# Weight sums spread over the products, a second out-projection in another product order, and mixing six steps behind its norm

## Chip, cores and metric

The kernel runs on one core of one Trainium2 chip. The metric is device time in microseconds (us); the time before is the median of three runs.

## What is computed

One decoder layer over 2048 tokens of width 1024, all in float32, and a final RMSNorm:

```python
h = rms_norm(x, norm_mix)
C, B, a, u, v, gA, gB = split(h @ w_in)                 # seven segments of 1024
y_a = B * causal_depthwise_conv(C * a, conv_w)
y_b = chunked_spatial_gating(gelu(u), gelu(v), ...)     # u * (tril(w_s) @ LN(v) + b) in chunks of 128
x = x + (sigmoid(gA) * y_a + sigmoid(gB) * y_b) @ w_out
h = rms_norm(x, norm_mlp)
x = x + square(relu(h @ w_ff1)) @ w_ff2
out = rms_norm(x, final_norm)
```

## The kernel before

**Tiling.** The tokens are two blocks of 1024. Every large product is done with one level of a Strassen-Winograd scheme: two by two quarters, seven products named 1 to 7 instead of eight. Each operand is split into a rounded part and a rest, and three matmuls of 128x128 against 512 columns stand for one exact product. A *step* is 12 such matmuls. For a product, sums of quarters of the weights (b11, b12, b21, b22) and of the activations are needed: those of the weights are made on VectorE (DVE) by `weight_sums` (L328), those of the activations by the jobs that write `h1d`, `md`, `h2d` and `hidd` to DRAM.

**Stages.** Per block: v projection (32 steps, `v_steps` L530), the other six segments (168 steps, `in_steps` L584). Then the out projection of block 0 and block 1 (28 steps each, `out_steps` L786), FF1 of both (112 each, `ff1_steps` L816) and FF2 of both (112 each, `ff2_steps` L850): 904 steps. `weave` (L997) interleaves the last four steps of a stage with the first four of the next. Here v.24 stands for step 24 of the v stage, out1 for the out projection of block 1, out0 for that of block 0.

**Order.** The order of TensorE (PE) and SyncE (SP, which issues the loads) is the program's; DVE, ScalarE (ACT) and GpSimd (POOL) are put in an order by the scheduler when the kernel is built, and then run their queues in that order. `drive` (L315) issues the loads of a step eight steps ahead and its preparation three steps ahead; jobs hung on a step by `at` (L974) come just before its matmuls. What stands in `with soon()` (L168) gets a priority 400 instructions earlier: weight sums, the splitting of weights into a unit (`wu`, four buffers) and the reading of PSUM banks. The splitting of activations (`hold<-rq`, `hold<-big`) has no such priority.

**Row products** (`row_steps` L684, used by out and FF2): nk steps per product (4 in out, 8 in each half of FF2), order `ROW_ORDER = "1265734"`. Products 1, 6, 7 and 4 add up in one set of four PSUM banks; product 2 has a set of its own; 5 and 3 share one in out0 and FF2 and have one each in out1 (`free`). After the last step of a product `read` (L739) adds the banks to rows of `x1`; a row that has all its sums is written to `x1d` by `finish`. PSUM has eight banks; the transposes and the mixing take from the same eight. The two weight quarters rows of a step are loaded with products 1 and 2, and product 6 makes all four weight sums.

**Jobs around it.** `ln_jobs` (L493) has `norm(i)`, the LayerNorm of 128 tokens of v and its split, and `mix(i, q)`, two groups of four matmuls (L461) on the result with reads by DVE (L521, L522); `at_mixes` (L989) hangs them on steps of v and of in. `h2_jobs(0)` (L1041, L1065) makes the normalised, transposed and summed input of block 0's FF1 during out1: `load(i)` of a row from `x1d`, `begin(i)` (square on ACT, power on POOL, scale on ACT), `turned(i)` (8 transposes on PE, L243, 8 evictions on ACT, L247), `sums(r)` (four sums on DVE into two tiles of the pool `extra`, which has two, and seven writes by POOL to `h2d`). FF1 of block 0 loads `h2d` from out1.20 on (L1057). Tiles of `hold` have fixed places named by letters; the rows `x1` of block 1 lie in places "5" (rows 0 to 3) and "3" (rows 4 to 7), and the first quarters of FF1 want all places "1" to "7" again (`quarters`, L280).

Of the kernel before, what the change touches and what calls it, by code (L numbers as in the profile page):

```python
# [38 lines left out]
def hybrid_block_kernel(  # L39
# [75 lines left out]
    def hf(dt=F32):  # L115
        return half.tile([P, HB], dt, tag="hf", name=nm("hf"))
# [21 lines left out]
    def sub(o, a, b):  # L138
        nc.vector.tensor_tensor(o, a, b, ALU.subtract)  # L139
# [11 lines left out]
    def split_new(src):  # L151
        u = wtile()
        split(u[:, 0, :], u[:, 1, :], src)
        return u
# [170 lines left out]
                f()  # L325
            st["run"]()

    def weight_sums(p, raw, st, after_2):  # L328

        b11, b12, b21, b22 = raw
        if p == "6":
            t = st["t"] = hf()
            sub(b11, b12, b11)
            sub(t, b22, b11)
            sub(b12, b22, b12)
            if after_2:
                sub(b21, b21, t)  # L340
        if p == "4" and not after_2:
            sub(st["t"], b21, st["t"])
        t = st.get("t")
        return {
            "1": b11, "6": t, "7": b12, "4": b21 if after_2 else t, "2": b21, "5": b11, "3": b22,
        }[p]

    def pair_steps(hq, cols, sink, done=None):

        raw, units, st = [], {}, {}

        def load():
            for n in range(2):
                for k in range(2):
                    t = rq()
                    src = cols[n][k * HB : (k + 1) * HB, :]  # L360
                    nc.sync.dma_start(
                        out=t.rearrange("p (k c) -> p k c", k=CH),
                        in_=src.rearrange("(k p) c -> p k c", p=P),
                    )
                    raw.append(t)

        def prep(p):
            b11, b21, b12, b22 = raw
            with soon():
                units[p] = split_new(weight_sums(p, (b11, b12, b21, b22), st, False))  # L370

        def run(p):
            first = p in "125"
            if first:
                st[GROUP[p]] = bank()
            ps = st[GROUP[p]]
            u, h = units.pop(p), hq[p]
            for k in range(CH):
                passes(
                    ps,  # L380
                    lambda a: u[:, a, k * P : (k + 1) * P],
                    lambda b: h[:, b, k, :],
                    first and k == 0,
                    k == CH - 1,
                    not first,
                )
            with soon():
                if p in "167":
                    st["s" + p] = hf()
                    copy(st["s" + p], ps)  # L390
                    return
                m, n = QUARTER[p]
                sink(m, n, ps, {"2": st["s1"], "3": st["s6"], "5": st["s7"], "4": None}[p])
            if p == ORDER[-1] and done is not None:
                done()

        return {
            p: step(load if p == "1" else nothing, lambda p=p: prep(p), lambda p=p: run(p))
            for p in ORDER
        }  # L400
# [281 lines left out]


    def row_steps(  # L684
        a_src, w, rows_of, nk, i0, x1, places, finish, free=False, late=False
    ):


# [3 lines left out]


        wrows, hid, banks, units, hraw = ({}, {}), {}, {}, {}, {}
        np_ = (nk + CH - 1) // CH

        def load(p, n):
            if p in "12":
                e = "12".index(p)
                if n % CH == 0:  # L700
                    wrows[e][n // CH] = held(places[e][n // CH], F32)
                r0 = rows_of(i0 + n)[e]
                nc.sync.dma_start(out=wrows[e][n // CH][:, n % CH, :], in_=w[r0 : r0 + P, :])
            t = rq()
            nc.sync.dma_start(out=t, in_=a_src[p][:, i0 + n, :])
            hraw[p, n] = t

        def prep(p, n):
            if n % CH == 0:
                hid[p, n // CH] = held(places[2]())  # L710
            h = hid[p, n // CH]
            split(h[:, 0, n % CH, :], h[:, 1, n % CH, :], hraw.pop((p, n)))
            w1 = wrows[0][n // CH][:, n % CH, :]
            raw = (w1[:, lo], w1[:, hi], None, None)
            if p != "1":
                w2 = wrows[1][n // CH][:, n % CH, :]
                raw = raw[:2] + (w2[:, lo], w2[:, hi])
            with soon():
                units[p, n] = split_new(weight_sums(p, raw, {}, True))

        def run(p, n):
            first = p in ("1253" if free else "125")
# [14 lines left out]
                )  # L737

            def read(r):  # L739
                for m, c in ROW_QUARTERS[p] if free or p != "5" else ((1, 1),):  # L740
                    t = x1[r + m * CH][:, c * HB : (c + 1) * HB]
                    with soon():
                        add(t, banks[p][r], t)
                    if p in "2734":
                        finish(r + m * CH, c)

            if late and p == "4" and n >= nk - CH:
# [15 lines left out]
                lambda p=p, n=n: prep(p, n),  # L763
                lambda p=p, n=n: run(p, n),
            )
            for p in ROW_ORDER
            for n in range(nk)
        ]

# [7 lines left out]
    def rotate(names):  # L777
        k = [0]

        def nxt():  # L780
            k[0] += 1
            return names[(k[0] - 1) % len(names)]

        return nxt

    def out_steps(blk, w_at, nxt, rows_at, free):  # L786
        x1, halves = [None] * (2 * CH), set()

        def finish(i, h):
# [11 lines left out]
            x1,  # L801
            (w_at[0], w_at[1], nxt),
            finish,
            free=free,
        )
        r0 = blk * BLK
# [167 lines left out]
    def at(steps, n, f):  # L974
        steps[n]["before"].append(f)
# [10 lines left out]
            if n % 2:  # L986
                at(steps, s + lag + 1, lambda r=n // 2: sums(r))

    def at_mixes(steps, n0, every, lag, jobs_of):  # L989
        for i in range(CH):  # L990
            at(steps, n0 + i * every, lambda i=i: jobs_of()[0](i))
            for q in range(2):
                at(steps, n0 + i * every + lag + q, lambda i=i, q=q: jobs_of()[1](i, q))

    phases = []

# [9 lines left out]
    for blk in blocks:  # L1006
# [16 lines left out]
        else:  # L1023
# [3 lines left out]
            for n, p in enumerate("675"):  # L1027
                bring(v[19 + 3 * n], *quarters(hq, h1d[blk], p))
            bring(inn[5], *quarters(hq, h1d[blk], "3"))
        at_mixes(v, 17, 3, 4, lambda blk=blk: late[blk, 0])  # L1030
        at_mixes(inn, 4, 2, 4, lambda blk=blk: late[blk, 1])
        if blk + 1 < NBLK:
            r0 = (blk + 1) * BLK
            jobs = quarter_jobs(
# [6 lines left out]
    def h2_jobs(blk):  # L1041
# [3 lines left out]

    nxt_g = rotate("673")
    outs = [
        out_steps(0, "16", rotate("7425"), (None, None), False),
        out_steps(1, "74", rotate("3162162"), ("5", "3"), True),
    ]  # L1050
    ff1s = [ff1_steps(blk, hqs[blk]) for blk in blocks]
    for blk in blocks:
# [10 lines left out]
                bring(s, load, prep)  # L1063

    load, begin, turned, sums = h2_jobs(0)  # L1065
    for n, s in enumerate((9, 9, 10, 11, 17, 17, 18, 19)):
        i = n // 2 + CH * (n % 2)
        at(outs[1], (2, 4, 4, 5, 8, 9, 10, 10)[n], lambda i=i: load(i))
        at(outs[1], (4, 6, 6, 7, 12, 12, 13, 13)[n], lambda i=i: begin(i))
        at(outs[1], s, lambda i=i: turned(i))  # L1070
        if n % 2:
            at(outs[1], s, lambda r=n // 2: sums(r))
    at_jobs(ff1s[0], 16, 10, 6, h2_jobs(1))
    at(outs[0], 8, no_more_z)
    for ph in outs + ff1s + [ff2_steps(blk, nxt_g) for blk in blocks]:
# [40 lines left out]
```

## Time and profile before

| | us |
|---|---|
| median of three runs | 2619.2 (2619.05 to 2620.46) |
| the profiled execution | 2617.14 |
| its span, first to last instruction | 2615.4 |
| PE busy | 2556.8 |
| DVE busy | 1853.1 |
| ACT busy | 1331.2 |
| POOL busy | 355.1 |
| granted TensorE clock, mean | 0.991 |

A busy time is the union of an engine's instructions; matmuls are pipelined and their ends are modelled. The granted clock is 1.00 at 2.4 GHz and 0.5 at 1.2 GHz, and a mean between them says how much of a stretch was at the lower one.

### The profile page before, as it was taken

How to read it: one execution, taken by the hardware profiler on the slowest of the kernel's cores; microseconds unless marked ns; L12 is line 12 of the kernel's file. 1: busy time of each engine (PE TensorE's matmuls, PEld its weight loads, DVE VectorE, ACT ScalarE, POOL GpSimd, SP SyncE). 2: the span in 40 equal slices, each digit the busy share in tenths (PEclk: the TensorE clock that was granted, in tenths of full speed). 3: DMA queues.
4: the chain of work that ended last, by engine and by line, in shares of the span. 5: the costliest groups of instructions: out<-in, count | busy, mean ns of one | idle time of the engine just before them, and what ended most of it. 6: DMA issues, size and time to landing. Idle time of an engine off the chain costs nothing.

```text
span 2615.4 us, 33276 instructions
## 1 busy us (share of the span) xinstructions
PE 2556.8 (98%) x11405; PEld 2112.7 (81%) x11405; DVE 1853.1 (71%) x3061; ACT 1331.2 (51%) x2377; POOL 355.1 (14%) x628
## 2 busy tenths in 40 slices
PE   9999999999999999999989999999999999999998
PEld 7778888888878888887768878888887888878887
DVE  6886776766887666777776666866668677685865
ACT  7444554445544344443666666755555444544444
POOL 1330111100330000000222223121121000000001
PEclk9999999999999999999999999999999999999999
DMA  6322344336332222354975555844449364563532
GB/s 218 93 76 86 122 133 136 121 111 223 113 93 85 69 89 69 101 184 141 370 256 195 190 185 197 274 150 158 145 149 338 129 209 122 204 242 118 183 127 77
DMA packets 291053, 410.65 MB, mean 157 GB/s; under 512 B 22804, under 2 KB 187716, under 8 KB 290884
## 3 DMA queue, kind: packets, MB, share of 16 engines
q1 hardware_dynamic: 247700, 276.90, 33.0%
q0 software_dynamic: 38576, 123.24, 13.1%
q10 hardware_dynamic: 4608, 8.39, 0.9%
q8 instruction: 89, 1.46, 0.2%
q14 instruction: 80, 0.66, 0.1%
HBM read 285.24 MB, written 123.21 MB: 156 GB/s over the span
## 4 chain that ended last, share of the span: by engine, by line
PE 32%; issue 9%; DMA 3%; DVE 3%; POOL 3%; ACT 1%; POOLq 0%; SPq 0%; ACTq 0%; DVEq 0%
PE ps L159 32%; POOL hidd L837 2%; DVE hold L139 1%; DMA rq<-in_w_ff_dram 1%; DMA rq<-hidd 1%; DVE wu L139 1%; DVE big L136 0%; DVE hf L139 0%; DMA h2d<-extra 0%; POOL h2d L260 0%; DMA hidd<-big 0%; DMA rq<-md 0%; PE ps L243 0%; DMA big<-h2d 0%; POOL st L873 0%
## 5 line engine op out<-in xcount | busy, mean ns | idle before, releaser
L159 PE MATMUL ps<-hold,wu 128*128 128x512 f32 x6720 | 1541.7, 390 | 11.7 <-ACT hf L145 8.9
L159 PEld LDWEIGHTS ps<-hold,wu 128*128 128x128 f32 x6720 | 1262.0, 188 | 277.1 <-ACT hf L145 11.5
L159 PE MATMUL ps<-wu,hold 128*128 128x512 f32 x4128 | 959.8, 393 | 18.8 <-DVE hold L139 12.4
L159 PEld LDWEIGHTS ps<-wu,hold 128*128 128x128 f32 x4128 | 779.6, 190 | 184.4 <-DVE hold L139 14.9
L139 DVE TENSOR_TENSOR wu<-rq,wu 128x512 fp32r<-128x512 f32 x464 | 319.9, 690 | 196.8 <-ACT wu L145 192.8
L145 ACT ACTIVATE wu<-rq 128x512 fp32r<-128x512 f32 x464 | 290.9, 627 | 308.3 <-PE ps L159 190.4
L145 ACT ACTIVATE wu<-hold 128x512 fp32r<-128x512 f32 x240 | 151.0, 631 | 280.3 <-PE ps L159 274.1
L145 ACT ACTIVATE hf<-ps 128x512 f32<-128x512 f32 x240 | 143.1, 596 | 262.5 <-PE ps L159 261.1
L139 DVE TENSOR_TENSOR wu<-hold,wu 128x512 fp32r<-128x512 f32 x240 | 165.4, 690 | 153.2 <-ACT wu L145 153.0
L139 DVE TENSOR_TENSOR wu<-hf,wu 128x512 fp32r<-128x512 f32 x200 | 137.8, 689 | 158.0 <-ACT wu L145 157.6
L145 ACT ACTIVATE wu<-hf 128x512 fp32r<-128x512 f32 x200 | 125.7, 629 | 174.1 <-PE ps L159 121.6
L139 DVE TENSOR_TENSOR hold<-rq,hold 128x512 fp32r<-128x512 f32 x280 | 181.2, 687 | 10.4 <-ACT hold L145 10.4
L837 POOL DMA_DIRECT2D hidd<-big x224 | 121.4, 542 | 459.5 <-ACT big L825 370.9
L145 ACT ACTIVATE hold<-rq 128x512 fp32r<-128x512 f32 x280 | 158.0, 619 | 48.7 <-DMA rq<-md 32.9
L136 DVE TENSOR_TENSOR big<-ps,hf 128x512 f32<-128x512 f32 x120 | 82.7, 689 | 60.1 <-PE ps L159 59.8
L139 DVE TENSOR_TENSOR rq<-rq,rq 128x512 f32<-128x512 f32 x160 | 110.2, 689 | 3.4 <-DMA rq<-in_w_ff_dram 0.3
L136 DVE TENSOR_TENSOR hf<-ps,hf 128x512 f32<-128x512 f32 x96 | 66.3, 690 | 62.1 <-PE ps L159 61.8
L873 POOL TENSOR_TENSOR st<-st,mhalf 128x1 f32<-128x1 f32 x16 | 14.5, 908 | 586.6 <-DVE st L872 586.6
L660 POOL DMA_DIRECT2D md<-big x56 | 30.5, 546 | 464.9 <-DVE big L136 454.1
L136 DVE TENSOR_TENSOR big<-ps,big 128x512 f32<-128x512 f32 (+1 forms) x148 | 90.5, 670 | 4.3 <-PE ps L159 2.9
L524 POOL DMA_DIRECT2D mixd<-hf x128 | 71.0, 555 | 115.5 <-DVE hf L522 63.8
L139 DVE TENSOR_TENSOR big<-big,big 128x512 f32<-128x512 f32 (+1 forms) x109 | 83.9, 771 | 1.9 <-ACT big L145 0.3
(108 smaller groups left out, 1585.0 us busy)
## 6 DMA issues: line engine op xcount, KB each, us to landing
rq<-in_w_in_dram SPq DMA_DIRECT2D x256, 256.0 KB, 2.9
hidd<-big POOLq DMA_DIRECT2D x224, 256.0 KB, 2.6
rq<-hidd SPq DMA_DIRECT2D x224, 256.0 KB, 3.9
rq<-in_w_ff_dram SPq DMA_DIRECT2D x128, 256.0 KB, 3.2
hold<-in_w_ff_dram SPq DMA_DIRECT2D x64, 512.0 KB, 6.6
big<-x1d SPq DMA_DIRECT2D x32, 512.0 KB, 7.3
md<-big POOLq DMA_DIRECT2D x56, 256.0 KB, 4.9
rq<-md SPq DMA_DIRECT2D x56, 256.0 KB, 8.5
```

The costliest lines, as they stand in the source:

```text
L136: nc.vector.tensor_tensor(o, a, b, ALU.add)
L139: nc.vector.tensor_tensor(o, a, b, ALU.subtract)
L145: nc.scalar.activation(o, a, AF.Copy)
L159: nc.tensor.matmul(ps, lhsT=stat_of(a), rhs=mov_of(b), start=first and n == 0, stop=last and n == 2, skip_group_check=goes_on,)
L524: nc.gpsimd.dma_start(out=mixd[blk][h + e][:, c0 : c0 + P], in_=o)
L660: nc.gpsimd.dma_start(out=md[blk][p][:, j, :], in_=src)
L837: nc.gpsimd.dma_start(out=hidd[blk][p][:, i, :], in_=src)
L873: nc.gpsimd.tensor_tensor(r, v, mhalf, ALU.pow)
```

## The change

Three things. `weight_sums` gets the order of the products and makes each sum at the product that first wants it: in ROW_ORDER b12-b11 moves from product 6 to 2, and b22-b12 from 6 to 7; in the order `ORDER = "1674253"` (the pairs of in and FF1, which had it before) b22-b12 moves from 6 to 7. out1 runs in ORDER instead of ROW_ORDER: its four products on one set of banks come first and one behind the other, the second weight row is loaded with product 6, and product 4 makes one sum more per step, since no tile is kept between products. Which product ends a quarter of the rows is worked out from the order. With it the jobs of `h2_jobs(0)` get other steps: rows are turned one per step, all sums are hung on out1.11 to 15 instead of 9 to 19. In v the norms go from steps 17, 20, 23, 26 to 16, 17, 18, 19, and the mixes from 21, 24, 27, 30 (and the next step of each) to 20, 22, 26, 28; in `in` the norms stay at 4, 6, 8, 10 and the mixes go from 8, 10, 12, 14 to 10, 12, 14, 16.

```diff
-    def weight_sums(p, raw, st, after_2):
+    def weight_sums(p, raw, st, order):
         b11, b12, b21, b22 = raw
-        if p == "6":
-            t = st["t"] = hf()
+        after_2 = order.index("2") < order.index("6")
+        if p == ("2" if after_2 else "6"):
             sub(b11, b12, b11)
-            sub(t, b22, b11)
+        if p == "6" or (p == "4" and "t" not in st and not after_2):
+            st["t"] = hf()
+            sub(st["t"], b22, b11)
+        if p == "6" and after_2:
+            sub(b21, b21, st["t"])
+        if p == "7":
             sub(b12, b22, b12)
-            if after_2:
-                sub(b21, b21, t)
...
     def row_steps(
-        a_src, w, rows_of, nk, i0, x1, places, finish, free=False, late=False
+        a_src, w, rows_of, nk, i0, x1, places, finish, order=ROW_ORDER, free=False, late=False
     ):
...
+        quarter_of = {p: q if free or p != "5" else ((1, 1),) for p, q in ROW_QUARTERS.items()}
+        adds = {
+            (m, c): [p for p in ORDER if (m, c) in quarter_of[p]]
+            for m in range(2)
+            for c in range(2)
+        }
         def load(p, n):
-            if p in "12":
-                e = "12".index(p)
+            if p in order[:2]:
+                e = order.index(p)
...
-                units[p, n] = split_new(weight_sums(p, raw, {}, True))
+                units[p, n] = split_new(weight_sums(p, raw, {}, order))
...
-                    if p in "2734":
+                    if all(p == q or order.index(q) < order.index(p) for q in adds[m, c]):
                         finish(r + m * CH, c)
...
-    def at_mixes(steps, n0, every, lag, jobs_of):
+    def at_mixes(steps, norms, mixes, jobs_of):
         for i in range(CH):
-            at(steps, n0 + i * every, lambda i=i: jobs_of()[0](i))
+            at(steps, norms[i], lambda i=i: jobs_of()[0](i))
             for q in range(2):
-                at(steps, n0 + i * every + lag + q, lambda i=i, q=q: jobs_of()[1](i, q))
+                at(steps, mixes[i] + q, lambda i=i, q=q: jobs_of()[1](i, q))
...
-        at_mixes(v, 17, 3, 4, lambda blk=blk: late[blk, 0])
-        at_mixes(inn, 4, 2, 4, lambda blk=blk: late[blk, 1])
+        at_mixes(v, (16, 17, 18, 19), (20, 22, 26, 28), lambda blk=blk: late[blk, 0])
+        at_mixes(inn, (4, 6, 8, 10), (10, 12, 14, 16), lambda blk=blk: late[blk, 1])
...
-        out_steps(0, "16", rotate("7425"), (None, None), False),
-        out_steps(1, "74", rotate("3162162"), ("5", "3"), True),
+        out_steps(0, "16", rotate("7425"), (None, None), ROW_ORDER, False),
+        out_steps(1, "74", rotate("3162162"), ("5", "3"), ORDER, True),
...
-    for n, s in enumerate((9, 9, 10, 11, 17, 17, 18, 19)):
-        i = n // 2 + CH * (n % 2)
-        at(outs[1], (2, 4, 4, 5, 8, 9, 10, 10)[n], lambda i=i: load(i))
-        at(outs[1], (4, 6, 6, 7, 12, 12, 13, 13)[n], lambda i=i: begin(i))
-        at(outs[1], s, lambda i=i: turned(i))
-        if n % 2:
-            at(outs[1], s, lambda r=n // 2: sums(r))
+    for i in range(2 * CH):
+        at(outs[1], (2, 2, 3, 3, 4, 5, 6, 7)[i], lambda i=i: load(i))
+        at(outs[1], (4, 4, 5, 5, 7, 8, 9, 10)[i], lambda i=i: begin(i))
+        at(outs[1], (6, 7, 8, 9, 11, 12, 13, 15)[i], lambda i=i: turned(i))
+        if i >= CH:
+            at(outs[1], (11, 12, 13, 15)[i - CH], lambda r=i - CH: sums(r))
```

## Rows read from the trace of the kernel before

**Rows 1.** The page, part 1: busy us (share of the span) and instructions of each engine.

```profile
PE 2556.8 (98%) x11405; PEld 2112.7 (81%) x11405; DVE 1853.1 (71%) x3061; ACT 1331.2 (51%) x2377; POOL 355.1 (14%) x628
```

**Rows 2.** Timeline of PE, undisturbed: start, us, instruction, count; FF2, then v of block 0.

```profile
2023.10 257.15 PE L159 MATMUL ps<-wu,hold 128*128 128x512 f32 x1133 [0.27 <-DVE hold L139]
...
82.80 1.11 PE L461 MATMUL ps<-big,big 128*128 128x256 f32 x8
83.75 2.91 PE L159 MATMUL ps<-wu,hold 128*128 128x512 f32 x12
```

**Rows 3.** Windows: stretch, length, busy us (instructions) by engine, clock, DMA share, GB/s.

```profile
93.00:107.00 14.00, 10.89 (x43) 8.91 (x42) 10.27 (x26) 6.44 (x15) 4.94 (x9) 0.76 0.32 94
171.00:191.00 20.00, 16.84 (x68) 13.71 (x69) 16.26 (x43) 6.67 (x10) 7.90 (x15) 0.83 0.19 59
745.00:762.00 17.00, 14.18 (x67) 11.57 (x68) 15.86 (x42) 6.32 (x10) 7.59 (x14) 1.00 0.21 67
1193.00:1206.00 13.00, 9.43 (x30) 7.23 (x29) 10.10 (x17) 2.52 (x4) 3.24 (x6) 0.74 0.77 240
1263.00:1270.00 7.00, 4.82 (x15) 3.81 (x15) 7.00 (x13) 3.86 (x7) 2.13 (x4) 0.76 1.03 401
1277.00:1296.00 19.00, 14.69 (x78) 11.60 (x77) 11.55 (x22) 17.84 (x46) 6.29 (x10) 1.00 1.03 402
1308.00:1333.00 25.00, 19.88 (x95) 15.87 (x93) 17.40 (x32) 21.81 (x53) 8.14 (x13) 0.93 0.50 160
1344.00:1380.00 36.00, 28.73 (x111) 22.56 (x110) 28.74 (x39) 18.19 (x26) 4.28 (x8) 0.91 0.99 351
2005.00:2027.00 22.00, 18.45 (x78) 13.96 (x77) 21.97 (x37) 8.36 (x15) 1.62 (x3) 1.00 0.90 330
2316.00:2332.00 16.00, 10.70 (x39) 8.34 (x38) 13.79 (x27) 6.74 (x14) 1.79 (x2) 0.79 0.66 218
```

**Rows 4.** Timeline of PE where it waited: in brackets us idle and what ended it.

```profile
98.52 2.93 PE L159 MATMUL ps<-wu,hold 128*128 128x512 f32 x6 [3.11 <-ACT big L569]
...
172.66 0.38 PE L461 MATMUL ps<-big,big 128*128 128x256 f32 x1 [1.73 <-ACT big L145]
174.17 1.86 PE L461 MATMUL ps<-big,big 128*128 128x256 f32 x7 [1.13 <-DVE big L139]
...
1265.29 15.46 PE L159 MATMUL ps<-wu,hold 128*128 128x512 f32 x60 [2.18 <-DVE big L136]
...
1370.03 10.32 PE L159 MATMUL ps<-hold,wu 128*128 128x512 f32 x37 [3.17 <-ACT hf L145]
...
2322.49 22.73 PE L159 MATMUL ps<-wu,hold 128*128 128x512 f32 x90 [5.30 <-DVE hold L139]
```

**Rows 5.** Timeline of DVE: reads of banks and a sum in out1, splits in FF2.

```profile
1264.46 2.48 DVE L136 TENSOR_TENSOR big<-ps,big 128x512 f32<-128x512 f32 x4
...
1341.21 0.69 DVE L139 TENSOR_TENSOR extra<-big,big 128x512 f32<-128x512 f32 x1 [3.28 <-DMA h2d<-extra]
...
2321.76 3.09 DVE L139 TENSOR_TENSOR hold<-rq,hold 128x512 fp32r<-128x512 f32 x5
```

**Rows 6.** Groups of DVE, 2294 to 2322 us: busy, mean ns, idle before them.

```profile
L139 DVE TENSOR_TENSOR hold<-hold,hold 128x512 f32<-128x512 f32 x6 | 4.1, 688 | 0.0
```

**Rows 7.** Groups of DVE, 1164 to 1198 us.

```profile
L139 DVE TENSOR_TENSOR hold<-hold,hold 128x512 f32<-128x512 f32 x2 | 1.4, 694 | 0.0
```

**Rows 8.** Timeline of ACT before the wait at 98.52.

```profile
96.84 1.06 ACT L145 ACTIVATE big<-big 128x1024 fp32r<-128x1024 f32 x1 [1.50 <-DVE big L504]
```

**Rows 9.** Waits of the SP queue, 1240 to 1380 us: total, times, longest.

```profile
SPq L288 <- DMA h2d<-big: 20.8, 2, 20.5
```

**Rows 10.** DMA issues: count, KB each, median us to landing.

```profile
x1d<-hold POOLq DMA_DIRECT2D x8, 512.0 KB, 8.5
```

**Rows 11.** The chain of waits, 1300 to 1375 us: start, us, what.

```profile
1333.72 7.47 DMA h2d<-extra
```

More of the change, by code (lines that the diff above doesn't have):

```diff
@@ L369, in prep @@
             with soon():
-                units[p] = split_new(weight_sums(p, (b11, b12, b21, b22), st, False))
+                units[p] = split_new(weight_sums(p, (b11, b12, b21, b22), st, ORDER))
         def run(p):
@@ L684, in row_steps @@
     def row_steps(
-        a_src, w, rows_of, nk, i0, x1, places, finish, free=False, late=False
+        a_src, w, rows_of, nk, i0, x1, places, finish, order=ROW_ORDER, free=False, late=False
     ):
         wrows, hid, banks, units, hraw = ({}, {}), {}, {}, {}, {}
-        np_ = (nk + CH - 1) // CH
+        quarter_of = {p: q if free or p != "5" else ((1, 1),) for p, q in ROW_QUARTERS.items()}
[4 more added lines that the diff above has]
+        }
         def load(p, n):
-            if p in "12":
-                e = "12".index(p)
+            if p in order[:2]:
+                e = order.index(p)
                 if n % CH == 0:
@@ L739, in read @@
             def read(r):
-                for m, c in ROW_QUARTERS[p] if free or p != "5" else ((1, 1),):
+                for m, c in quarter_of[p]:
                     t = x1[r + m * CH][:, c * HB : (c + 1) * HB]
@@ L765, in row_steps @@
             )
-            for p in ROW_ORDER
+            for p in order
             for n in range(nk)
@@ L784, in rotate, with out_steps @@
         return nxt
-    def out_steps(blk, w_at, nxt, rows_at, free):
+    def out_steps(blk, w_at, nxt, rows_at, order, free):
         x1, halves = [None] * (2 * CH), set()
@@ L803, in out_steps @@
             finish,
+            order=order,
             free=free,
```

## Prediction

> **What bounds the kernel now.** I read the page's part 1 first: PE is busy 98% of the span, DVE 71%, ACT 51% [rows 1]. So time can only come out of PE's gaps and out of the stretches in which its clock was lower. The undisturbed pace is in PE's timeline: 1133 matmuls in 257.15 us, 0.227 us each, so a step of 12 takes 2.72 us; one mix adds 0.95 us (82.80 to 83.75) [rows 2]. 904 steps at that pace are some 2460 us.
>
> Then I went through PE's waits and laid a window over each place at which a step took longer than that; apart from the first 55 us and from 2.9 us in FF1 of block 0, which the change doesn't touch, they all lie where the change works [rows 3, 4]. What a window lost is its length less its matmuls at 0.227 us, where it has nothing else: out0 13 - 30 x 0.227 = 6.2; start of out1's second product 7 - 15 x 0.227 = 3.6; out1 into FF1 36 - 111 x 0.227 = 10.8; FF2 of block 0 22 - 78 x 0.227 = 4.3; FF2 of block 1 16 - 39 x 0.227 = 7.1. In the last one idle is 5.3 us and the clock's share (1 - 0.79) x 16 = 3.4, so about 54% of the clock's share came on top of the idle time. With that for the mixed windows: v of block 0 3.1 + 0.54 x 3.4 = 4.9; mixing in block 0 3.2 + 1.8 = 5.0; in block 1 2.8; out1's first turns 4.3; its later turns 5.1 + 0.9 = 6.0. Together 55 us, which is all that this change could give.
>
> **FF2 sums (11.4 us).** In the window of block 1 PE waits 5.30 us for a split of activations on DVE [rows 4]. DVE has no idle time there; it makes weight sums of product 6, which have priority, while product 2 wants its activations, and the five splits come only at 2321.76 [rows 5]. The change adds and drops no sum in FF2. It puts one of four per step behind: 8 per half. Six of those lie in the 28 us before the splits [rows 6]; DVE starts one every 0.60 us (2.48 us for four, [rows 5]), so the splits come 3.6 us earlier, 4.8 if the two before count as well. A wait of 0.5 to 1.7 us is left of 5.3. I take no fall of the clock with it, since out1's first turns idle 4.3 us in 19 at a clock of 1.00 [rows 3]; 6.0 of 7.1 us return. The same 3.6 us cover the 3.55 us idle of block 0 (22 - 18.45): 4.0 of 4.3. **Gain 10**; bounds 0 (the scheduler makes the sums as early as before, since they keep their priority) and 11.4.
>
> **out0 (6.2 us).** It gets the same spreading, but with four steps per product everything lies within the 400 instructions of priority, and in the trace only two of the moved sums lie in the 34 us before its wait [rows 7]. Two times 0.60 us leave, if at all. **Gain 1**; bounds -2 (the sums fall into the crunch) and 6.2.
>
> **Mixing in `in` (7.8 us).** Mix 3 waits for the split of its norm, first on ACT, then on DVE: 1.73 + 1.13 us [rows 4]. The norms stay; mix 3 goes two steps later, which is 2 x (2.72 + 0.95) less the two mixes that no longer lie before it, 2 x 0.95: 5.4 us later, and DVE has two mixes fewer to read before that norm. 2.9 us were missing. What is late next: the reads of the last mixes now meet the convolution on DVE, which is busy 16.3 of 20 and 15.9 of 17 us there [rows 3]. **Gain 6.5**; bounds 2 and 7.8.
>
> **Mixing in v (4.9 us).** At v.24 PE waits 3.11 us for evictions on ACT (L569) [rows 4]; ACT's queue had the split of norm 2 before them, itself waiting for DVE [rows 8]. With norm 2 at step 18 that obstacle is gone. But four mixes and all four norms now come before step 24 instead of three mixes and three norms, and DVE is nearly full there (10.3 of 14 us with the wait in it, [rows 3]); the eight tiles that four norms want at once also don't fit beside the rest of the pool of 12, so norm 2 waits for mix 0 anyway. **Gain 1** for both blocks; bounds -7 (both blocks wait at step 24 for reads on DVE) and 4.9.
>
> **out1 (24.7 us).** Its parts:
> - *Second product.* Before, product 2 waited for four banks of out0, 2.18 us until a read by DVE [rows 4]. Now product 6 goes on in the banks of product 1, so it wants the four reads behind those: 2.39 us later [rows 5], less the two sums that leave (1.2). Costs 1.5 more; bounds -4 and +3.6.
> - *Two more hand-overs* (6 to 7, 7 to 4) on the same banks, which there were not before. PE comes back to the first bank 2.0 us (9 matmuls) after finishing it, 2.9 with a turn between, and an add takes 0.6: free if DVE's queue is short, else up to 3.6 each as above. I take 1.5 each: -3; bounds -7.2 and 0.
> - *Turns.* Before, transposes waited for banks that DVE had to read and for ACT, busy 17.8 of 19 us and 21.8 of 25 [rows 3]. Now products 1, 6, 7, 4 leave the other four banks to them and rows come one per step; but ACT has the same squares, scalings and evictions of eight rows in 12 steps instead of 16. Of 4.3 + 6.0 I give back 6.5; bounds 0 and 10.
> - *Into FF1.* SP stands 20.8 us for `h2d` [rows 9], because the last sums hang on step 19; what queues behind it are the loads of FF1's weights and quarters, and PE waits 3.17 us at 1370 [rows 4]. The sums now end four steps (10.9 us) sooner and the turns before them lose less, so nearly all of that wait goes. Late next: rows 0 to 3 lie in place "5", end now with out1's last product, and their writes take 8.5 us to land [rows 10]; with two splits (about 3.5 us) that is 12 to 13 us, and FF1's first use of place "5" comes 4 steps = 10.9 us after. Gain 10.8 - 2.5 = 8; bounds -5 and 10.8.
> - The four extra sums are 2.4 us of DVE and no step of PE waits for them alone; 0.
>
> **Gain 10**; bounds -16 and 24.
>
> Two places of the Trainium skill speak against this order. "PSUM — Partial Sum Buffer", section "Summary: rules for kernel authors", wants reads of PSUM to lie in another bank than the running matmuls; by it every hand-over costs the full wait. The trace has that wait once (2.18 us, [rows 4]; 3.6 with the clock); with it at each of three hand-overs out1 would gain 10 - (10.8 - 4.5) = 4. "TensorE: Matmul & The Clock Gate", section "A second HAM failure mode: psum-queue depth-cycling", says that short repeated waits for banks make the clock fall and recover again and again; here 4.3 us idle in 19 kept a clock of 1.00, but 2.2 us in 7 went with 0.76 [rows 3], so the trace shows both.
>
> **Sum.** 10 + 1 + 6.5 + 1 + 10 = 28.5. The profiled execution is 2617.14 us (span 2615.4 and 1.7 around it), 2.1 below the median. 2617.1 - 28.5 + 2.1 = 2590.7; I say 2591.
>
> **Rivals.**
> - *A, the forecast:* 2591, its own range 2577 to 2603. Chance 0.52.
> - *B, all waits go:* out0 too, and hand-overs cost nothing: 2619.2 - 52 = 2567 (2560 to 2576). For it: each place lost little, and each has one wait as its cause. Against: DVE and ACT are nearly full in v and out1. Chance 0.14.
> - *C, out1 gives back what it takes:* hand-overs at 3.6 each and ACT-bound turns; left are FF2 and `in`, 16 us: 2603 (2600 to 2612). Chance 0.14.
> - *E, spreading does nothing:* the sums keep their priority and their place in DVE's queue, FF2 waits as before: 2591 + 10 = 2601 (2596 to 2606). For it: six of them ran before the splits although their product comes much later [rows 6]. Against: product 7's come eight steps behind 6's. Chance 0.10.
> - *D, slower:* the four sums of rows lie close now, and each wants both tiles of `extra`, which the writes of the one before must first leave: 7.47 us on the chain [rows 11]. DVE's queue stands meanwhile (3.28 us at 1341, [rows 5]) with the bank reads behind it, which the same-bank products now need within 2 us. Three such waits passed on in full cost 22.4, three falls of the clock 3 x 1.8 = 5.4, hand-overs 4.5, and FF1's start is late again (no 8): out1 -27.8 - 4.5 + 6.5 = -26 against the +18.5 of the rest: 2627. It decides from about 5 us per wait, where the total is zero. The Trainium skill, "TensorE: Matmul & The Clock Gate", says in its part on queue depths that DVE's queue is strictly first in, first out; the trace agrees, 3.28 us idle with reads due. Chance 0.10.
>
> **How the numbers follow.** What a measurement here can tell from no change is about 0.2%, 5.2 us. A, B, C and E are faster by more than that save for the upper edges of C; D is split between slower and no change. Faster 0.87, same 0.05, slower 0.08. The range leaves out the lower half of B, D and the edges: 2565 to 2612.
>
> **What would show it.** FF2: no wait over 1 us at its ninth step in block 1, clock 1.00, and the sums `hold<-hold,hold` after the splits; E if they stay before them. `in`: no wait of L461 for a split. v: a wait at v.24 now ended by DVE instead of ACT would be my doubt come true. out1: SP's wait for `h2d` below 10 us; waits at out1.4, 8 and 12 ended by DVE's reads (`hold<-ps`), of 1 to 4 us; D if DVE is idle before `extra` for more than 5 us each time; a wait at FF1's eighth step ended by the split into place "5". My sum is wrong first if the scheduler's new order of DVE and ACT, which I can't see, puts other work before the reads.

## Result and the profile after

| | before | after |
|---|---|---|
| median, us | 2619.1 (2615.9 to 2620.5) | 2631.8 (2630.9 to 2633.5) |
| ratio to before | | 1.0051 (95% interval 1.0034 to 1.0068) |
| span of the profiled execution, us | 2615.4 | 2629.2 |

The change makes the kernel 12.7 us slower. Forecast were 28.5 us less. No engine has more to do, DVE's four sums and 4 us aside; the page's part 1 of after against [rows 1]:

```profile
PE 2556.7 (97%) x11405; PEld 2112.0 (80%) x11405; DVE 1857.3 (71%) x3065; ACT 1333.4 (51%) x2377; POOL 350.0 (13%) x628
```

So the loss is idle time and clock again, and it can be laid out by stage. PE runs its steps in the same order in both kernels, so the start of a step of after less that of the same step of before, taken at the ends of the stages, says what each stage gained or lost between the two profiled executions ("by step starts" below; 13.7 in all, where the medians differ by 12.7; minus is faster, and "out1 and into FF1" goes up to FF1's step 24):

| stage | forecast | after less before, us |
|---|---|---|
| v, block 0 (with the start) and 1 | -1 | -1.3, +2.5 |
| `in`, block 0 and 1 | -6.5 | -3.8, -1.2 |
| out0 | -1 | -1.1 |
| out1 and into FF1 | -10 | **+11.7** |
| rest of FF1, block 0 | 0 | +3.8 |
| FF2, block 0 and 1 | -10 | **+4.0, -0.9** |

Two terms carry the miss: out1 by 21.7 us, FF2 by 13.1. The windows of after, in the order and with the columns of [rows 3]; lines are shifted (L464, L525 and L364 are before's L461, L522 and L361, L713 the load of `md` in `row_steps`, L705 there):

```profile
84.00:107.00 23.00, 19.51 (x89) 15.74 (x88) 20.71 (x54) 12.03 (x23) 10.54 (x18) 0.93 0.38 113
166.00:187.00 21.00, 21.00 (x109) 17.97 (x108) 19.49 (x50) 7.44 (x11) 9.86 (x19) 1.00 0.30 93
...
1188.00:1201.00 13.00, 9.43 (x42) 7.48 (x41) 11.10 (x18) 2.12 (x4) 3.25 (x6) 1.00 0.68 205
1257.00:1264.00 7.00, 1.41 (x7) 0.89 (x5) 7.00 (x13) 3.22 (x6) 2.13 (x4) 0.76 1.04 403
1271.00:1290.00 19.00, 12.53 (x60) 10.31 (x59) 9.53 (x19) 13.09 (x27) 6.14 (x6) 0.82 1.00 382
1303.00:1328.00 25.00, 17.91 (x75) 14.08 (x73) 15.88 (x26) 20.65 (x53) 8.38 (x16) 0.86 0.58 185
...
2016.00:2038.00 22.00, 15.81 (x59) 12.24 (x58) 19.50 (x34) 7.94 (x14) 0.00 (x0) 0.84 0.81 292
2333.00:2349.00 16.00, 11.02 (x42) 8.68 (x41) 14.14 (x26) 5.61 (x10) 1.47 (x1) 0.89 0.62 201
```

Mixing in `in` now leaves PE no idle time (21.00 of 21.00). In out1 all three windows got worse: the fifth step's idles 5.6 of 7 us, and the first turns have 60 matmuls and transposes where 78 were. The waits behind them, from PE's timeline of after (as [rows 4]):

```profile
90.31 1.20 PE L464 MATMUL ps<-big,big 128*128 128x256 f32 x4 [1.70 <-DVE hf L525]
...
190.40 4.87 PE L159 MATMUL ps<-hold,wu 128*128 128x512 f32 x20 [2.01 <-ACT hf L145]
...
1263.89 7.41 PE L159 MATMUL ps<-wu,hold 128*128 128x512 f32 x24 [5.59 <-DVE hold L136]
1277.74 1.97 PE L243 MATMUL ps<-ident,big 128*128 128x128 f32 x8 [6.45 <-ACT big L236]
...
1309.77 2.15 PE L243 MATMUL ps<-ident,big 128*128 128x128 f32 x8 [4.90 <-ACT big L247]
...
1358.00 5.06 PE L159 MATMUL ps<-hold,wu 128*128 128x512 f32 x11 [6.14 <-DVE hold L139]
...
2027.43 17.87 PE L159 MATMUL ps<-wu,hold 128*128 128x512 f32 x68 [5.37 <-DVE hold L139]
...
2339.50 10.84 PE L159 MATMUL ps<-wu,hold 128*128 128x512 f32 x40 [4.98 <-DVE hold L139]
```

*1263.89* is the hand-over from product 1 to 6. DVE's timeline shows what it waits for: the four reads of out0's last banks, a split, then the four reads of product 1, of which the first ends the wait:

```profile
1260.07 2.47 DVE L136 TENSOR_TENSOR big<-ps,big 128x512 f32<-128x512 f32 x4
1262.47 0.68 DVE L139 TENSOR_TENSOR wu<-hf,wu 128x512 fp32r<-128x512 f32 x1
1263.07 2.47 DVE L136 TENSOR_TENSOR hold<-ps,hold 128x512 f32<-128x512 f32 x4
...
1272.94 0.14 DVE L215 TENSOR_SCALAR st<-st 128x1 f32<-128x1 f32 x1
```

*1277.74* is the first turn. The last line above belongs to it: row 0's square is done on ACT at 1264, but the small operation of its norm on DVE (0.14 us of work) comes only at 1272.94. In before it came at the same time, but there the first turn was three steps later:

```profile
1272.85 0.15 DVE L215 TENSOR_SCALAR st<-st 128x1 f32<-128x1 f32 x1
```

ACT's timeline of after has the square and then the scaling, which stood for POOL's power behind that operation:

```profile
1262.94 1.06 ACT L235 ACTIVATE junk<-big 128x1024 bf16<-128x1024 f32 x1
...
1276.54 1.15 ACT L236 ACTIVATE big<-big,st 128x1024 f32<-128x1024 f32 x1 [3.49 <-POOL st L217]
```

*1358.00* is FF1's first step, which wants the rest of quarter 1 from DVE. SP's wait for `h2d` before it (20.8, [rows 9]) is gone, as forecast, but SP is no earlier: it now stands longer (at `md` 36.4 us against 16.5) ahead of the loads of `md` (L713) and of FF1's weights (L364), until the splits of raw activations and weights on DVE give their buffers back, and reaches `h2d` at 1340.87 (in before at 1312.36). Its waits from 1230 to 1385 us (total, times, longest):

```profile
SPq L713 <- DVE hold L139: 36.4, 6, 20.2
SPq L364 <- DVE hold L139: 19.7, 5, 13.4
SPq L364 <- DVE wu L139: 18.1, 3, 11.3
```

### The profile page after: what moved, and what is told of

Same layout as the page of the kernel before. It is cut to its first block, busy times and chain, and to the rows that moved or that the text cites. A ratio compares the mean times of both kernels' runs of the same rounds, so it can differ in the third digit from the quotient of the medians.

```text
span 2629.2 us, 33292 instructions
## 1 busy us (share of the span) xinstructions
PE 2556.7 (97%) x11405; PEld 2112.0 (80%) x11405; DVE 1857.3 (71%) x3065; ACT 1333.4 (51%) x2377; POOL 350.0 (13%) x628
## 4 chain that ended last, share of the span: by engine, by line
PE 37%; issue 6%; DMA 2%; DVE 2%; POOL 2%; ACT 1%; SPq 0%; POOLq 0%; ACTq 0%; DVEq 0%
PE ps L159 37%; POOL hidd L846 1%; DMA rq<-hidd 1%; DVE hold L139 1%; DVE wu L139 1%; DMA hidd<-big 0%; DMA hold<-in_w_ff_dram 0%; POOL h2d L260 0%; DMA big<-h2d 0%; DVE big L136 0%; POOL st L882 0%; ACT big L247 0%; DMA h2d<-extra 0%; DVE hf L139 0%; POOL st L217 0%
## 5 line engine op out<-in xcount | busy, mean ns | idle before, releaser
L145 ACT ACTIVATE hold<-rq 128x512 fp32r<-128x512 f32 x280 | 159.0, 621 | 55.4 <-DMA rq<-md 36.4
L136 DVE TENSOR_TENSOR big<-ps,hf 128x512 f32<-128x512 f32 x120 | 82.5, 688 | 62.8 <-PE ps L159 62.0
L136 DVE TENSOR_TENSOR hf<-ps,hf 128x512 f32<-128x512 f32 x96 | 66.2, 690 | 62.5 <-PE ps L159 62.4
L136 DVE TENSOR_TENSOR big<-ps,big 128x512 f32<-128x512 f32 (+1 forms) x148 | 90.0, 666 | 4.3 <-PE ps L159 2.9
L834 ACT ACTIVATE big<-big 128x512 f32<-128x512 f32 x128 | 80.5, 629 | 2.6
```

The lines of the kernel that those rows point to most:

```text
L136: nc.vector.tensor_tensor(o, a, b, ALU.add)
L145: nc.scalar.activation(o, a, AF.Copy)
L834: nc.scalar.activation(t, t, AF.Square)
```

## The parts one by one

The first question is whether the parts cost what the stages say, or whether one part's new order of the queues spoils another stage. Each part was put alone into the kernel before.

**Out1's order and job steps alone** (e1; the sums of `weight_sums` and all mixing stay):

```diff
-        out_steps(1, "74", rotate("3162162"), ("5", "3"), True),
+        out_steps(1, "74", rotate("3162162"), ("5", "3"), ORDER, True),
...
-        at(outs[1], s, lambda i=i: turned(i))
+        at(outs[1], (6, 7, 8, 9, 11, 12, 13, 15)[i], lambda i=i: turned(i))
```

> Only the out projection of block 1 in its new product order with the new steps of its row jobs; weight sums all at product 6 and mixing as before. Theory P (each part costs at its own place what the changed kernel's trace shows there): out1 until FF1's fifth step loses about 12 us against before, all else as before: 2631. Rival Q (the parts act through the order in which the scheduler puts DVE and ACT over the whole kernel, so that a part alone costs something else): out1 alone loses less than 6 us, below 2625.

2631.4 us, ratio 1.0045 (1.0030 to 1.0060). This part alone costs nearly all that the change costs, and at the same places; PE's waits from 1236 to 1400 us:

```profile
PE ps L159 <- DVE hold L139: 11.3, 3, 6.5
PE ps L159 <- DVE hold L136: 6.4, 1, 6.4
PE ps L243 <- ACT big L247: 5.1, 2, 4.9
PE ps L243 <- ACT big L236: 3.7, 1, 3.7
```

**The weight sums alone** (e2; `weight_sums` as in the change, out1 and mixing as before):

> Only the weight sums spread over the products; out1 in the old order, mixing as before. Theory P: FF2 loses 3 us, FF1 of block 0 between 0 and 4, out0 gains 1.3: 2620 to 2625; the sums of product 7 still run before the splits in FF2, because their priority lifts them over the eight steps by which they were moved. My prediction's mechanism: FF2's waits of 3.6 and 5.3 us go, 2608. Rival Q: FF2 unchanged or better, since its losses came from elsewhere: 2619 or less.

2621.4 us, ratio 1.0008 (0.9999 to 1.0018): no change that can be measured. In FF2 PE still waits 9.9 us in two places.

**Mixing in v and `in` alone** (e3):

```diff
+        at_mixes(v, (16, 17, 18, 19), (20, 22, 26, 28), lambda blk=blk: late[blk, 0])
+        at_mixes(inn, (4, 6, 8, 10), (10, 12, 14, 16), lambda blk=blk: late[blk, 1])
```

> Only the mixing: norms and mixes of v and of in on the new steps. Theory P: in gains 4.5 in each block (its wait of 2.9 us for a split goes, a new one of 2.0 us at in.20 comes), v gains 1 in block 0 and loses 1.5 in block 1: 4 us faster, 2615. Rival Q: no gain, 2619 or more.

2617.5 us, ratio 0.9994 (0.9984 to 1.0003).

**Mixing in `in` alone** (e4; v stays):

> Only the mixes of in two steps later; v as before. Theory P: as e3 without v, 2614 (v of block 1 waits no more, v of block 0 has its wait of 3.1 us again). Rival R (the wait at in.20 comes from the mixing of v through the queues): in.20 doesn't wait and the kernel is 9 us faster, 2610.

2614.6 us, ratio 0.9983 (0.9974 to 0.9993), the one part that pays. The wait at `in`.20 (2.2 us in this run, in both blocks) comes with `in`'s mixing alone, so v's isn't its cause. The two medians put v's mixing at 2.9 us of loss, and the trace shows where: in block 1, which had no wait at step 24, PE now waits for reads by DVE (L522 in e3, L525 in after) in v.

The parts add up to the whole within 2 us (11.5 + 1.6 - 2.4 = 10.7 against 12.7), so they can be treated apart.

## FF2: who comes first on DVE

**The kernel before, with priority for FF2's splits of activations** (e5):

```diff
-            split(h[:, 0, n % CH, :], h[:, 1, n % CH, :], hraw.pop((p, n)))
+            with soon() if nk > CH else nullcontext():
+                split(h[:, 0, n % CH, :], h[:, 1, n % CH, :], hraw.pop((p, n)))
```

> The kernel before, but in FF2 alone the splits of activations get the priority that the weight sums have; the number of instructions is the same. Theory S (FF2 waits because the sums of later weights have priority over the splits of activations, so that spreading them over products changes nothing while they keep it): no wait over 1 us is left at FF2's steps 8 and 9 of block 1 (5.30 before) and at step 9 of block 0, no fall of the clock there; gain 7 to 11, so 2608 to 2612 us. Rival T (DVE simply has too much work in these 25 us, and an order of it only moves the wait): PE waits as long, at another step for a weight unit wu, 2619 us; the sums that are pushed back would then stand before the next units.

2607.4 us, ratio 0.9954 (0.9941 to 0.9967). No wait above 0.15 us is left in FF2; the two windows, to be held against the last two of [rows 3]:

```profile
2005.00:2027.00 22.00, 22.00 (x99) 18.23 (x98) 21.21 (x36) 8.30 (x14) 1.62 (x3) 1.00 1.04 408
2309.00:2325.00 16.00, 16.00 (x73) 13.24 (x72) 15.93 (x27) 6.78 (x13) 0.00 (x0) 1.00 0.60 228
```

DVE does as much as before and is as full; only the order within it changed. Theory S holds, rival T (too much work) falls. The 11.4 us that the forecast saw in FF2 were there: by step starts 12.6 came back.

**The spreading, with product 7's sum out of the priority** (e6):

```diff
+            behind = p == "7" and nk > CH
+            s7 = weight_sums(p, raw, {}, ROW_ORDER) if behind else None
             with soon():
-                units[p, n] = split_new(weight_sums(p, raw, {}, ROW_ORDER))
+                units[p, n] = split_new(s7 if behind else weight_sums(p, raw, {}, ROW_ORDER))
```

> The spreading of the weight sums alone (as in e2_sums), and in FF2 the sum of product 7 is taken out of the priority; its split keeps it. Theory S: the sums of product 7 (four before the splits in block 0, five in block 1) now run behind the splits, 0.6 us each, so 5.37 falls to 3 or less in block 0 and 4.98 to 2 in block 1: 2614 to 2618 us against 2621.4 for the spreading alone. Rival T: waits stay near 5 us each, 2621 us. By the forecast on record this is what the spreading should have done by itself.

2613.3 us, ratio 0.9975 (0.9963 to 0.9987). So in block 0 it was the priority that held the moved sums in front: from 2000 to 2018 us DVE makes five of product 7's sums in e2, the line below, and none in e6.

```profile
L139 DVE TENSOR_TENSOR hold<-hold,hold 128x512 f32<-128x512 f32 x5 | 3.4, 686 | 0.0
```

Without it FF2 of block 0 has no wait any more (5.0 us by step starts), as the forecast wanted of the spreading. Block 1 keeps its wait, so there the moved sums weren't the cause:

```profile
PE ps L159 <- DVE hold L139: 5.2, 1, 5.2
```

There the splits come at 2319.68, seven in a row, behind product 6's sums and the rows of block 0's final norm, which this edit doesn't move.

## out1: order, turns and hand-over

**The new order with the old steps** of `load`, `begin`, `turned` and `sums` (e7; e1 with the loop of before over the jobs):

> out1 in the new order of products, with the turns, loads and sums of the rows at the steps of the kernel before. Theory M (two separate costs: the order costs the hand-over at out1.4, 6.4 us of wait instead of 2.18, and the first quarters of FF1 come late because rows lie in place 5 until out1's last product; the new steps cost the wait for row 0's norm and that for ACT at the fifth turn): the waits at out1.6 and 13 (3.71 and 4.89 in e1_out1) are gone, the one at out1.4 stays at 5 to 6.5, the one in FF1's second step stays at 4 or more; 2622 to 2628 us. Rival N (the order is the cause of all, the turns only show it): 2631. Rival O (the order is free, the new steps cost all): 2619.

2625.7 us, ratio 1.0029 (1.0020 to 1.0039). The wait for row 0's norm shrinks to 0.89, the hand-over stays at 5.17, and SP waits for `h2d` again (19.9). The order costs about 7 us, the steps the other 5: theory M.

**The first four turns later** (e8, on e1):

```diff
-        at(outs[1], (6, 7, 8, 9, 11, 12, 13, 15)[i], lambda i=i: turned(i))
+        at(outs[1], (9, 9, 10, 10, 11, 12, 13, 15)[i], lambda i=i: turned(i))
```

> As e1_out1, but the first four turns at out1.9, 9, 10 and 10 in place of 6 to 9; the rest and all sums stay. Theory M: row 0's norm is ready by then, the wait of 3.71 at out1.6 is gone, and the turns wait less altogether; the hand-over at out1.4 stays (6.4); 2626 to 2629 against 2631.4. Rival (ACT and DVE are full over the whole stretch, so that a later start only gathers the wait at the fifth to eighth turn): 2631 to 2634, with the wait at out1.13 grown by what out1.6 lost.

2633.4 us, ratio 1.0056 (1.0039 to 1.0073): theory M falls here, the rival is right. The norm's wait is down to 0.89, but two turns at a step meet ACT's evictions of the rows before:

```profile
1295.93 4.21 PE L243 MATMUL ps<-ident,big 128*128 128x128 f32 x16 [6.99 <-ACT big L247]
```

A turn that starts later gains nothing while ACT's queue stands behind the norms.

**Out1 alone, with priority for the small operations of the norms** (e11, on e1):

```diff
-        nc.vector.tensor_scalar(v, ssq, 1.0 / D, EPS, ALU.mult, ALU.add)
-        r = small(1)
-        nc.gpsimd.tensor_tensor(r, v, mhalf, ALU.pow)
+        with soon():
+            nc.vector.tensor_scalar(v, ssq, 1.0 / D, EPS, ALU.mult, ALU.add)
+            nc.gpsimd.tensor_tensor(r, v, mhalf, ALU.pow)
```

> As e1_out1 (out1's order and job steps alone), but the small operations of a row's norm, on DVE and POOL, get priority in all row norms. Theory M (turned(0) at out1.6 waits because DVE's small operation L215 runs at 1272.9 although row 0's square was done at 1262.9): it runs within 3 us of the square, the wait for L236 at out1.6 (3.71 in e1_out1, 6.45 in the change) is gone, and out1's later turns start with a shorter queue on ACT: 2624 to 2628 us against 2631.4. Rival (ACT is full, the wait only moves to the evictions L247): 2630 to 2633.

2626.1 us, ratio 1.0022 (1.0012 to 1.0031). DVE's timeline has the operation now right behind the reads, 1.5 us after the accumulated square (done at 1266.15), and PE waits for no scaling any more:

```profile
1265.21 2.48 DVE L136 TENSOR_TENSOR hold<-ps,hold 128x512 f32<-128x512 f32 x4
1267.61 0.15 DVE L216 TENSOR_SCALAR st<-st 128x1 f32<-128x1 f32 x1
```

By step starts out1 costs 3.7 instead of 10.9; by the medians e11 is 5.3 below e1. Two operations, the one on DVE 0.15 us long, in the wrong place of two queues were worth 5 to 7 us. Not all of it is the wait at the first turn (3.71 in e1): the one at the hand-over, too, is 4.74 instead of 6.40 with the new order of the queues.

**Product 2 back behind product 1** (e13, on e8):

```diff
-        out_steps(1, "74", rotate("3162162"), ("5", "3"), ORDER, True),
+        out_steps(1, "74", rotate("3162162"), ("5", "3"), "1267453", True),
```

> As e8_turn_later, but out1's products in the order 1267453: product 2 behind product 1 on banks of its own, as before the change; 6, 7 and 4 still follow one another. Theory H (the wait at out1.4 is the hand-over: product 6 goes on in the banks of product 1, whose four reads stand behind the four of out0): the wait falls from 5.19 to about 2.2, the kernel of before's, with less of the lower clock; the turns, which begin at out1.9, are unchanged: 2627 to 2630 us against 2633.4. Rival (the wait is due to DVE's queue at that point, whatever product comes next): 4 us or more at out1.4 and 2632 to 2635; or it comes back in full at out1.8, where product 6 now wants product 1's banks.

2626.4 us, ratio 1.0021 (1.0011 to 1.0032), 7 less than with the hand-over. The wait is the one of before, for out0's banks (L136 into `big`, not into `hold`), and it does not come back at out1.8, though product 6 still goes on in product 1's banks there, nor at the hand-overs from 6 to 7 and 7 to 4:

```profile
1261.41 16.68 PE L159 MATMUL ps<-wu,hold 128*128 128x512 f32 x60 [2.84 <-DVE big L136]
```

So going on in the same banks costs little by itself; what costs is that at out1.4 eight reads are due at once, four of them another stage's.

**Out1 alone, with priority for the splits of quarters** (e12, on e1: `split` in `quarters` within `soon()`):

> As e1_out1, but the splits of the quarters of the activations (`hold<-big`, those that FF1's first steps want) get priority, in all stages that load quarters. Theory S: FF1's first step no longer waits for the rest of quarter 1 on DVE (6.50 in e1_out1): 2 or less, and 2.80 at its sixth step falls too: 2625 to 2628 us. Rival V (the quarters come late from DRAM, so priority finds nothing to do; SP loads them only at 1340): wait of 4 or more, now ended by the load or by ACT: 2630 to 2632.

2632.3 us, ratio 1.0043 (1.0027 to 1.0059). The 6.50 at FF1's first step falls to 1.82, now ended by ACT's half of the split, and 3.6 us of out1's loss are gone by step starts; but the end of FF1 of block 0 loses 7 more. The execution profiled here is the slowest of four (2637.1), so that this loss is in the others too is not shown. The loads of quarters stand in every stage, and which of the queues that shift lost the time was not separated. So the late split is shown as the cause of that wait, but moving it alone pays nothing that the median shows.

## Both causes at once, and a faster kernel

**The whole change, with priority for all splits of activations in the row products** (e9; e5's edit without its condition):

> The whole change, and the splits of activations in out0, out1 and FF2 with the priority of the weight sums. Theory S (these splits are late because they alone have no priority): the waits of 5.37 and 4.98 in FF2 go, 11 to 12 us; in out1 SP's waits for buffers of raw activations (36.4 us at the loads of md) fall below 15, and FF1's first loads start earlier than 1340: 2612 to 2620 us against 2631.8 for the change. Rival T (DVE is full in out1, and what is put ahead there pushes back the reads of banks): FF2's gain comes, but out1 grows by 3 or more: 2622 to 2626.

2610.4 us, ratio 0.9961 (0.9946 to 0.9976). FF2's waits are gone (12.6 us), 5.5 more than in the change come back in out0. SP's wait for raw buffers falls to 13.6, and it reaches the loads of `h2d` at 1303.98 instead of 1340.87; but there it stands for the rows' sums:

```profile
SPq L288 <- DMA h2d<-extra: 36.7, 2, 19.5
SPq L364 <- DVE wu L139: 21.2, 5, 8.0
SPq L713 <- DVE hold L139: 13.6, 6, 7.0
```

FF1's first step waits 1.97 instead of 6.14, yet out1 as a whole still loses 10.4 (11.7): the waits at out1.4 (5.87) and out1.6 (6.45) are untouched.

**The whole change with both priorities (e14), and before with both and `in`'s mixing (e15):**

> The whole change, with priority for the splits of activations in the row products (e9_after_acts, 2610.4) and for the small operations of the norms (e11_out1_norm, 5.3 us less than e1_out1). If the two add up, the wait of 6.45 at out1.6 is gone, the one of 5.87 at out1.4 stays: 2604 to 2607 us. Rival (ACT is full: the wait for the norm becomes one for evictions L247): 2609 to 2612.

> The kernel before with the mixing of `in` of the change and the same two priorities as e14_after_norm; out1's order and steps, v's mixing and the weight sums stay those of before. If out1's new order costs something even with the queues in a good order (the hand-over of 5.87 at out1.4 that this one hasn't): 2597 to 2602 us, some 5 us below e14_after_norm. Rival (without the late splits and norms the new order is as good or better, as the forecast said): within 2 us of e14_after_norm or above it.

e14: 2604.5 us, ratio 0.9936 (0.9921 to 0.9950). e15: 2595.6 us, ratio 0.9902 (0.9887 to 0.9916), the fastest kernel of this study. The two gains add up. PE's waits from 1236 to 1400 us, first with the change's out1, then with that of before:

```profile
PE ps L243 <- ACT big L247: 8.0, 4, 3.0
PE ps L159 <- DVE hold L136: 5.9, 1, 5.9
PE ps L159 <- DVE hold L139: 4.1, 3, 2.2
PE ps L159 <- ACT hf L145: 2.1, 1, 2.1
PE ps L243 <- ACT big L236: 0.6, 1, 0.6
```

```profile
PE ps L159 <- ACT hf L145: 6.6, 3, 5.0
PE ps L243 <- ACT big L247: 3.3, 4, 1.4
PE ps L243 <- DVE hold L136: 3.2, 3, 1.5
PE ps L243 <- DVE st L216: 2.3, 1, 2.3
PE ps L159 <- DVE big L136: 1.6, 1, 1.6
PE ps L159 <- DVE hold L139: 0.7, 1, 0.7
```

With the queues in good order the change's out1 still costs 5.6 us by step starts and v's mixing some 3. In out1 it is the hand-over (5.9 against 1.6) and the splits of activations (4.1 against 0.7), less ACT's share (2.1 against 6.6). The turns (L243) wait as long in both, 8.6 against 8.8 us; only what they wait for differs, ACT's evictions L247 in the one, mostly DVE in the other. So a turn at every step is then no dearer, but of the 6.5 us forecast for it these waits show next to nothing (9.4 us in before).

**Before, with `in`'s mixing and FF2's priority only** (e10):

> The kernel before with the one part of the change that paid, the mixing of `in` two steps later (e4_mix_in, 4.5 us), and FF2's splits of activations with priority (e5_ff2_acts, 11.5 us). If the two places are separate, the gains add up: 2603 us (2600 to 2606). Rival: the new order of the queues between them takes back one of them: 2607 to 2611.

2601.3 us, ratio 0.9926 (0.9913 to 0.9940); the two places are separate. The gain, 0.74%, is that of the two alone, 0.17% and 0.46%, or a little more.

## Why the prediction was wrong

- **What bounds the kernel** was read rightly: the change moved idle time and clock. e15 took 24.6 us of the 55, and by step starts they came out of `in`, out0, out1 and FF2, where the windows lay.
- **FF2 sums, 10 us forecast, -3 came.** The step that failed is "so the splits come 3.6 us earlier". It counted how many sums leave the 28 us and took it that their time goes to the splits of the step that wants them. In block 0 the sums did not leave: the bound 0 of that step named the cause, that the sums "keep their priority", rival E had it at 0.10, and e6 shows it. Against E stood "product 7's come eight steps behind 6's"; the 400 instructions of priority reach further. One of these sums, at 2018.88, still lies between the first split and the reads, and the wait grew. In block 1 four of the six [rows 6] did leave (two are left from 2311 to 2339 us of after), yet the splits aren't earlier for it: the wait moved from step 8 to step 9, 5.30 to 4.98. Ahead of the splits there now stand one more row of block 0's final norm and 1.7 us (0.6 in before) in which DVE itself waits, for a load of weights and for POOL. That b12-b11 moves forward, to product 2, had no place in the sum either. e5 shows what the splits lacked in both blocks: priority.
- **out0, 1 us:** 1.1 by step starts, within what two executions differ by.
- **Mixing in `in`, 6.5 us:** the mechanism was right (no wait for the split of a norm, 21.00 of 21.00 us busy), 5.0 came by step starts, 4.5 by e4's ratio. The difference is a new wait of 2.0 at `in`.20 for ACT in each block, for which the sum had no term. The text had named the place as "late next", reads that meet the convolution on DVE; the copy on ACT that PE waits for came behind an operation that needed such a read, done at 188.52 between two pieces of the convolution.
- **Mixing in v, a gain of 1 us forecast:** a loss of 1.2. The doubt written there came true, though at v.22 and v.23 instead of v.24: DVE's reads (L525) end the waits, 5.7 us in six over both blocks.
- **Second product and hand-overs, -1.5 and -3:** the first hand-over's wait went from 2.18 to 5.59, within the bound of 3.6 more but not the value taken; with the clock the step lost 4.2 us in e1. Of the 3.4 more, 3.0 are the way from the first of out0's reads to the first of product 1's (1260.07 to 1263.07; 2.39 in the forecast, which left out the split between them). I took off 1.2 for two sums that leave, but nothing came earlier: against the steps out0's reads are 0.4 later than in before. The two others cost nothing that a wait shows, so rival C's 3.6 each is wrong. The rule on which bank to read while matmuls run (the Trainium skill, "PSUM — Partial Sum Buffer", "Summary: rules for kernel authors") has no price in it; that every hand-over costs the full wait was my reading, and the trace has a wait at one of the three.
- **Turns, +6.5:** the failed step is "rows come one per step; but ACT has the same ... in 12 steps instead of 16". The look at ACT's share missed that a row's norm passes through DVE and POOL before ACT may scale it. In before that small operation ran at 1272.85, when the first turn was at out1.9; the change put the turn at out1.6 and the operation stayed at 1272.94. e11 shows it: 5 to 7 us. The clock fell with it, to 0.82 and 0.86 in the two windows that had 1.00 and 0.93 [rows 3]. What the Trainium skill, "TensorE: Matmul & The Clock Gate", "A second HAM failure mode: psum-queue depth-cycling", tells of short repeated waits is not shown by it: nearly all of the first window's idle time (6.45 of 6.47 us), and most of the second's (4.90 of 7.09), is one long wait.
- **Into FF1, +8:** SP's wait for `h2d` did end, as forecast, and nothing came of it: SP's queue is one line, and the loads of `md` and of weights ahead of it waited for buffers that late splits hold. "So nearly all of that wait goes" left out what else stood in that queue. That place "5" would be late next was not shown: the long wait is at FF1's first step, for the split of quarter 1.
- **Rival D** gave 2627 and 0.10, nearest to the result, by another mechanism: the waits for `extra` on DVE are 0.50, 0.86 and 0.37 in after, not 7.47. That DVE's strict order hands a wait on to the reads and splits behind, which D rested on, is seen in e5, e6 and e11, where little more than that order was changed; only what stood in front was something else.
- **The rest of FF1, not in the sum:** +3.8 in after, but between 0.7 and 11.7 in all fifteen experiments, also where out1, v and the sums were left alone (3.4 in e4). It is mostly the same waits for ACT with another fall of the clock (below), and one at FF1's step 106, 1.4 to 2.7 us, that after and all fifteen have and before alone has not. So the profile of before is a favourable one here, and that the change causes any of the 3.8 is not shown.

## What to carry to other kernels

When work is moved in a program whose queues a scheduler orders, first ask what priority the moved work keeps and which of its neighbours have none: an idle PE behind a full DVE was cured by ordering (11.5 us), not by having less ahead. A chain that crosses three engines is priced by its slowest place in a queue, not by its 0.15 us of work, so look up when each link ran before moving its consumer forward. And a wait that ends in one queue is worth only what the next thing in that queue leaves of it.

## What the runs showed of the hardware

The same wait does not always bring the same clock. In `in` of block 0, e5 leaves everything as in before, and PE's two waits are those of [rows 4] to the hundredth (1.73 and 1.13), but its window has the clock at 1.00 where [rows 3] has 0.83, and by step starts the stage is 2.6 us shorter:

```profile
171.00:191.00 20.00, 17.24 (x81) 14.13 (x82) 18.88 (x49) 7.97 (x13) 9.18 (x18) 1.00 0.21 65
...
172.26 0.38 PE L461 MATMUL ps<-big,big 128*128 128x256 f32 x1 [1.73 <-ACT big L145]
173.77 1.09 PE L461 MATMUL ps<-big,big 128*128 128x256 f32 x7 [1.13 <-DVE big L139]
```

The other way round in FF1, near 1525: behind a wait of 2.90 in before the clock of the 10 us around its end is 1.00, behind one of 3.02 in e5 it is 0.66 (before, then e5):

```profile
1525.00:1535.00 10.00, 8.52 (x37) 7.05 (x38) 7.91 (x13) 6.40 (x12) 2.74 (x5) 1.00 0.34 116
1523.00:1533.00 10.00, 8.04 (x23) 6.41 (x24) 6.37 (x10) 5.33 (x9) 2.20 (x4) 0.66 0.29 107
```

My surcharge of 54% of the clock's share is therefore a mean over luck, and differences of 2 to 3 us between two single profiles say nothing at such a place; the medians have to.
